# Attention products stored as high and low parts, the output projection's first units begun at step 9 of the last pair of heads, and an entrance's sum of squares kept in PSUM

## The chip, the core and the metric

One core of a Trainium2 chip. A core has a matrix engine (TensorE, PE in the profile; its weight loads are shown as PEld), three engines for elementwise work (VectorE or DVE, ScalarE or ACT, GpSimd or POOL), a queue engine (SyncE or SP), and 16 DMA engines that move data between HBM and the on-chip memories: SBUF, which holds operands, and PSUM, into which TensorE accumulates. Each engine runs its own instructions in one fixed order, and semaphores tie the engines together. The metric is the device time of one execution in microseconds (us); lower is better.

## What is computed

A decoder trunk of two layers over 1040 tokens (16 learned meta tokens and 1024 of the input) of width 1024, in float32. Layer 0 is a state-space mixer and a gated feed-forward network with a short causal convolution (conv FFN); then keys and values are projected once; layer 1 is stick-breaking attention over 16 heads and another conv FFN. The part of the reference around the change:

```
def _rmsnorm(x, g):
    x32 = x.astype(jnp.float32)
    y = x32 * lax.rsqrt(jnp.mean(x32 * x32, axis=-1, keepdims=True) + NORM_EPS)
    return (y * g.astype(jnp.float32)).astype(x.dtype)
...
        logits = jnp.einsum('bthd,bshd->bhts', q[:, t0:t1], k[:, :t1]).astype(jnp.float32) * scale
...
        log_keep = jnp.where(visible, jax.nn.log_sigmoid(-logits), 0.0)
        later = lax.cumsum(log_keep, axis=3, reverse=True) - log_keep
        log_w = jnp.where(visible, jax.nn.log_sigmoid(logits) + later, -jnp.inf)
        w = jnp.exp(log_w).astype(v.dtype)
        outs.append(jnp.einsum('bhts,bshd->bthd', w, v[:, :t1]))
...
            o = _stick_breaking_attention(q, k_shared, v_shared).reshape(b, L, SB_WIDTH)
            h = h + o @ sb_w_o[j]
        h = h + _conv_ffn(_rmsnorm(h, ffn_norm[layer]), ffn_w_up[layer], ffn_conv_w[layer],
                          ffn_conv_b[layer], ffn_w_down[layer])
```

## The kernel before

**Products in two parts.** Each float32 operand x of the large products is kept as a high part (x rounded, type F32R) and a low part (x minus the high part), and each product is three matmuls: high by high, low by high, high by low (lines 209, 210 and 211; their names, such as `acc<-o,wh`, tell what is multiplied). ScalarE makes the high part by a copy, VectorE or GpSimd the low part by a subtraction (line 102 is GpSimd's helper, which cuts a tile into pieces of 256 columns).

**Attention** runs over 8 pairs of heads; a pair has 18 steps, one for each block row i of 116 tokens and each column tile jj of 348 up to the diagonal. In a step `weigh` makes on TensorE the logits lg (line 1651), on ScalarE two sigmoids of them, kp and bt (lines 1652 and 1653), on GpSimd the masks of a diagonal block (1657), on VectorE a running product over kp (the scan, 1662) and bt times it (1663). The logits of all steps go to the same PSUM tile, so the next lg waits until ScalarE's bt has read it. Two steps later (LAG) `turn` transposes bt on TensorE (wT, 1685) and ScalarE copies it out (wt, 1691). When the block rows of a visit are through (a pair has four visits: (0, 1, 2), (3, 4, 5), (6, 7), (8,)), `values` multiplies them by v into PSUM (po, 1708), ScalarE copies po to the SBUF tile o (1710), and at three of the four visits stores o to DRAM (`o_d`, 1712) by a DMA that is issued on ScalarE's own queue. Between these, each step holds part of the next pair's projections of q, k and v (pj), whose weight parts come from ScalarE (wh, 1552) and VectorE (wl, 1553), and whose results VectorE reads (k, 1575; klo, 1587; qs, 1603; v, 1618).

**The last pair** has no next pair to project for. From its step 9 on (`BEHIND`) each step takes one piece of the generator `o_blocks`, which begins the output projection with the pairs that are done (the first four): it fetches o's rows from DRAM (`fetch_o`, line 1796, on SyncE's queue), splits them in two parts (`split_o`: ScalarE 1802, VectorE 1803), splits w_o's tiles (`parts`: ScalarE 1820, GpSimd 102), fetches rows of the residual stream h, and in `unit(f, j)` multiplies 128 output features f by token block j (12 matmuls) and adds the sum to h (VectorE, 538). The first unit stands in step 12. After the last pair the remaining units run, and `o_proj` fetches and splits the other four pairs' o for the entrance.

**An entrance** (`enter_ffn`) ends a projection and starts the FFN: for each of two token tiles it adds the last products to h, squares each of the 8 feature tiles on ScalarE (sq, 1061) and sums the squares, so that one matmul with a matrix of ones (ms) gives each token's sum. `square_row` adds them on VectorE (1063), m tiles to a sum: all in one for the first tile, none for the second. There is one entrance in each layer; the sums stand at 780 us and at 2111 us.

Of the kernel before, what the change touches and what calls it, by code (L numbers as in the profile page):

```python
# [8 lines left out]
F32 = mybir.dt.float32  # L9
F32R = mybir.dt.float32r  # L10
AF = mybir.ActivationFunctionType
ALU = mybir.AluOpType

P = 128
D = 1024
KD = D // P
META = 16
SEQ = 1024
L = META + SEQ
# [3 lines left out]
TT = [(0, 348), (348, 348), (696, 344)]  # L23
TW = 352
QW = 1056
# [35 lines left out]
PAIRS = 8  # L61
# [1 line left out]
NPOOL = 3  # L63
DT0 = 0
LAG = 2
BEHIND = 9
VISITS = (0, 1, 2), (3, 4, 5), (6, 7), (8,)

NW = 8
# [36 lines left out]
class Trunk:  # L106
# [950 lines left out]

    def square_row(self, ms, h, f, s0, n, m):

        q = self.tmp("sq")[:, :n]  # L1060
        self.nc.scalar.activation(q, h[f][:, HB + s0 : HB + s0 + n], AF.Square)
        if f % m:
            self.nc.vector.tensor_tensor(self.squares, self.squares, q, op=ALU.add)
        elif m > 1:
            self.squares = q
        if m == 1:
            self.last_ms = self.nc.tensor.matmul(ms[:, :n], self.ones, q, start=f == 0, stop=f == KD - 1, skip_group_check=True)
# [625 lines left out]
    def values(self, p, visit, wt, v, o, od):  # L1693


        nc = self.nc
        first, last = visit[0], visit[-1]
        j, c0 = first // 3, first % 3 * CB
        end = CH[last][0] + CH[last][1]
        n = end - CH[first][0]  # L1700
        each = wt[0][0].shape[1]
        po = self.ex("po")
        order = [*range(first, last + 1), *range(first - 1, -1, -1)]
        for x, c in enumerate(order):
            t0 = max(c - first, 0) * CB
            q, r = divmod(c, each)
            for a in range(2):
                nc.tensor.matmul(po[64 * a : 64 * a + 64, t0:n], v[: CH[c][1], c, 64 * a : 64 * a + 64], wt[a][q][: CH[c][1], r, t0:n],  # L1708
                                 start=x == 0, stop=x == last, skip_group_check=True)
        nc.scalar.activation(o[:, c0 : c0 + n], po[:, :n], AF.Copy)  # L1710
        if last % 3 == 2:
            nc.scalar.dma_start(od[p, :, TT[j][0] : end], o[:, : TT[j][1]])

    def attention(self, u, pool, hd):


        od = self.dp.tile([PAIRS, P, L], F32, tag="o_d", name="o_d")
        steps = [(i, jj) for i in range(9) for jj in range(i // 3, -1, -1)]

        halves = {(own, n0 + h): (kind, j, h) for own, n0, kind, j in (  # L1720
# [8 lines left out]
        def flush(n):  # L1729
            while ready:  # L1730
                p, visit = ready.pop()
                if visit[0] % 3 == 0:
                    os[p] = self.tmp("o")
                self.values(p, visit, wts.pop((p, visit)), pairs[p].v, os[p], od)
            if len(turns) > n:
                p, i, jj, bt = turns.pop(0)
                visit = next(v for v in VISITS if i in v)
                if (p, visit) not in wts:
                    wts[p, visit] = self.weight_tiles(visit)
                self.turn(i, jj, bt, wts[p, visit], visit[0])  # L1740
                if jj == 0 and i == visit[-1]:
                    ready.append((p, visit))
# [46 lines left out]
    def fetch_o(self, od, p, x):  # L1789


        g = FFN[1]
        s0, m = g.part(x)
        t = self.Q("o", F32R)
        hi, lo = t[:, :m], t[:, QW // 2 : QW // 2 + m]
        self.nc.sync.dma_start(lo.bitcast(F32), od[p, :, g.at + s0 : g.at + s0 + m])
        return hi, lo

    def split_o(self, hl):

        hi, lo = hl
        self.nc.scalar.activation(hi, lo.bitcast(F32), AF.Copy)
        self.nc.vector.tensor_tensor(lo, lo.bitcast(F32), hi.bitcast(F32), op=ALU.subtract)

    def o_blocks(self, hd, od):


        nc, a, g = self.nc, self.a, FFN[1]
        at, n, K = g.at - g.lead, g.n + g.lead, PAIRS // 2
        self.ho = h = [None] * KD  # L1810
        ws, rows = {}, [None, None]

        def fetch_w(f):
            ws[f] = self.wp.tile([P, 1024], F32, tag="w32", name=self.nm("w32"))
            nc.sync.dma_start(ws[f][:, : K * P], a["w_o_f"][f][:, : K * P])

        def parts(f):
            w32 = ws[f][:, : K * P]
            wh, wl = (self.wp.tile([P, 1024], F32R, tag=t, name=self.nm(t))[:, : K * P] for t in ("wh", "wl"))
            nc.scalar.activation(wh, w32, AF.Copy)  # L1820
            pieces(nc.gpsimd, wl, w32, wh.bitcast(F32), ALU.subtract)
            ws[f] = wh, wl

        def fetch_h(f):
            h[f] = self.Q("h")
            nc.sync.dma_start(h[f][:, :n], hd[f][:, at:])

        def unit(f, j):
            w = ws[f]
            self.accumulate(h, f, *g.span(j), lambda i, f: tuple(x[:, i * P : i * P + P] for x in w), rows[j // 2], HB, self.mm, g.part(j // 2)[0])  # L1830

        rows[0] = [self.fetch_o(od, p, 0) for p in range(K)]
        fetch_w(0)
        fetch_w(1)
        yield
        for hl in rows[0][:2]:
            self.split_o(hl)
        yield
        for hl in rows[0][2:]:
            self.split_o(hl)  # L1840
        parts(0)
        yield
        rows[1] = [self.fetch_o(od, p, 1) for p in range(K)]
        fetch_h(0)
        fetch_h(1)
        unit(0, 0)
        yield
        parts(1)
        unit(0, 1)
        yield  # L1850
        for hl in rows[1][:2]:
            self.split_o(hl)
        unit(1, 0)
        yield
        for hl in rows[1][2:]:
            self.split_o(hl)
        unit(1, 1)
        fetch_w(2)
        fetch_h(2)
        yield  # L1860
        order = [(0, 2), (0, 3), (1, 2), (1, 3)] + [(f, j) for f in range(2, KD) for j in range(4)]
        for x, (f, j) in enumerate(order):
            if x % 4 == 2 and x // 4 + 2 < KD:
                parts(x // 4 + 2)
                if x // 4 + 3 < KD:
                    fetch_w(x // 4 + 3)
                    fetch_h(x // 4 + 3)
            unit(f, j)
            yield

    def o_proj(self, od, blocks, pool):


        a = self.a
        first = PAIRS // 2
        for _ in blocks:
            pass

        def part(p, x):
            hl = self.fetch_o(od, p, x)  # L1880
            self.split_o(hl)
            return hl

        ops = [part(p, 0) for p in range(first, PAIRS)]
        ws = [self.load_wd(a["w_o"][first + i], i < 2) for i in range(4)]
        second = [part(p, 1) for p in range(first, PAIRS)]
        return self.enter_ffn(1, self.ho, [(ws, lambda: ops), (ws, lambda: second)], pool)


# [173 lines left out]
```

## Time and profile before

| what | value |
|---|---|
| three executions | 2862.64, 2856.94 and 2861.96 us; median 2861.96 us |
| profiled execution | 2864.79 us, of which the span of its instructions is 2862.9 us |
| mean granted TensorE clock | 0.996 of full speed |
| instructions | 56393 |
| ScalarE's stores of o (line 1712) | 24, 0.33 us of issue each, from 1563.9 to 2078.2 us |
| fetches of o (line 1796) | 16, of some 257 KB each, from 2014.3 to 2086.3 us |
| splits of o: ScalarE (1802), VectorE (1803) | 16 and 16, 0.63 and 0.69 us each (medians) |
| sums of squares (line 1063) | 14, of 0.43 us (median), the longest 8.88 us |

A row of the timeline reads: start in us, duration in us, engine, line, operation, what is written <- what is read, shape, how many in a row; in brackets the idle time of the engine just before it, and what it waited for. A "q" behind an engine's name is its sequencer, which issues DMAs. A row of windows gives, for a stretch of time, its length and the busy us (and instructions) of PE, PEld, DVE, ACT and POOL, the granted clock of TensorE, the busy share of the DMA engines and GB/s. A row of one line's instructions gives least/median/greatest duration in ns. A row of waits gives who waits, for whom, us in total, times, and the longest.

### The profile page before, as it was taken

Reading aid. Unit: us, or ns where it says so; the run is one execution under the profiler, and the core shown is the slowest. Engines: PE = TensorE matmul, PEld = TensorE weight load, DVE = VectorE, ACT = ScalarE, POOL = GpSimd, SP = SyncE. Lnnn points to the kernel's source line nnn. Section 1 sums busy time; section 2 is a strip of 40 time slices with the busy share of each in tenths; the row PEclk is TensorE's granted clock in tenths of the full one; section 3 lists DMA queues with packets and bytes.
Section 4 is the critical chain, followed back from the end, with each engine's and each line's share of the span. In section 5 each row is a group of like instructions: output and inputs, shape, how many; then the busy total and the mean of one; then the engine's idle time right before and its main releaser. Section 6 shows DMA issues by size and latency. Waiting matters only on the chain.

```text
span 2862.9 us, 56393 instructions
## 1 busy us (share of the span) xinstructions
PE 2813.9 (98%) x21251; PEld 2695.1 (94%) x21251; DVE 2073.6 (72%) x3920; ACT 1589.3 (56%) x3093; POOL 1577.6 (55%) x2144
## 2 busy tenths in 40 slices
PE   8999999999999999999999999999899999999998
PEld 7989999999999999999999999999799999999888
DVE  5676666668597666677886888878669776766776
ACT  5555454543265656555335777777636555555433
POOL 2366455643529888868853111122254888885881
PEclk9999999999999999999999999999999999999999
DMA  4343334333413222245132222221432222225331
GB/s 119 88 112 103 107 86 134 108 132 101 126 59 97 81 79 79 80 156 174 43 128 77 66 69 62 63 59 47 136 107 76 80 80 78 81 82 184 111 104 67
DMA packets 136237, 273.32 MB, mean 95 GB/s; under 512 B 15924, under 2 KB 68285, under 8 KB 135965
## 3 DMA queue, kind: packets, MB, share of 16 engines
q1 hardware_dynamic: 130340, 258.55, 28.9%
q0 software_dynamic: 2048, 6.49, 0.6%
q10 hardware_dynamic: 3576, 4.67, 0.5%
q8 instruction: 168, 2.75, 0.4%
q14 instruction: 105, 0.85, 0.1%
HBM read 203.58 MB, written 51.16 MB: 89 GB/s over the span
## 4 chain that ended last, share of the span: by engine, by line
PE 89%; DVE 5%; ACT 2%; issue 2%; POOL 1%; DMA 0%; DVEq 0%; SPq 0%; ACTq 0%; POOLq 0%
PE p L211 10%; PE p L209 10%; PE p L210 10%; PE acc L209 8%; PE acc L211 8%; PE acc L210 8%; PE pj L209 8%; PE pj L210 7%; PE pj L211 7%; PE po L1708 2%; PE lg L1651 2%; PE wT L1685 2%; PE y L810 1%; PE S L799 1%; PE y L812 1%
## 5 line engine op out<-in xcount | busy, mean ns | idle before, releaser
L102 POOL TENSOR_TENSOR wl<-w,wh 128x256 fp32r<-128x256 f32 x760 | 678.9, 923 | 359.8 <-ACT wh L196 216.8
L209 PE MATMUL pj<-uh,wh 128*128 128x348 f32 (+2 forms) x1536 | 500.7, 327 | 2.1 <-DVE xbc L339 1.4
L210 PE MATMUL pj<-ul,wh 128*128 128x348 f32 (+2 forms) x1536 | 494.8, 322 | 0.8 <-DVE ul L320 0.8
L211 PE MATMUL pj<-uh,wl 128*128 128x348 f32 (+2 forms) x1536 | 492.1, 320 | 0.0
L209 PE MATMUL p<-bh,fh 128*128 128x262 f32 (+1 forms) x1408 | 400.8, 285 | 3.9 <-DVE p L1235 3.7
L211 PE MATMUL p<-bh,fl 128*128 128x262 f32 (+1 forms) x1408 | 400.8, 285 | 2.0 <-POOL fl L102 2.0
L210 PE MATMUL p<-bl,fh 128*128 128x262 f32 (+1 forms) x1408 | 397.5, 283 | 0.0
L102 POOL TENSOR_TENSOR fl<-x,fh 128x256 fp32r<-128x256 f32 x352 | 263.9, 782 | 190.3 <-ACT fh L1172 140.0
L210 PE MATMUL p<-bl,wh 128*128 128x262 f32 (+1 forms) x1040 | 295.5, 284 | 0.7 <-DVE bl L1096 0.7
L209 PE MATMUL p<-bh,wh 128*128 128x262 f32 (+1 forms) x1040 | 295.2, 284 | 0.8 <-ACT ft L1232 0.8
L211 PE MATMUL p<-bh,wl 128*128 128x262 f32 (+1 forms) x1040 | 294.3, 283 | 0.0
L209 PEld LDWEIGHTS pj<-uh,wh 128*128 128x128 f32 x1536 | 288.7, 188 | 4.5 <-ACT xbc L336 1.7
L210 PEld LDWEIGHTS pj<-ul,wh 128*128 128x128 f32 x1536 | 289.3, 188 | 2.4 <-DVE ul L320 1.4
L339 DVE SCALAR_TENSOR_TENSOR c<-p,params,c 128x260 f32<-128x260 f32 (+1 forms) x528 | 248.2, 479 | 57.5 <-ACT c L336 50.9
L211 PEld LDWEIGHTS pj<-uh,wl 128*128 128x128 f32 x1536 | 288.7, 188 | 0.1
L209 PEld LDWEIGHTS p<-bh,fh 128*128 128x128 f32 x1408 | 267.8, 190 | 4.8 <-DVE p L1235 4.1
L211 PEld LDWEIGHTS p<-bh,fl 128*128 128x128 f32 x1408 | 265.9, 189 | 2.9 <-POOL fl L102 2.7
L210 PEld LDWEIGHTS p<-bl,fh 128*128 128x128 f32 x1408 | 267.4, 190 | 0.1
L1232 ACT ACTIVATE ft<-p 128x262 f32<-128x262 f32 (+1 forms) x352 | 133.2, 382 | 178.9 <-DVE p L1235 110.9
L210 PE MATMUL acc<-gl,wh 128*128 128x260 f32 (+1 forms) x672 | 214.1, 320 | 0.0
L211 PE MATMUL acc<-gh,wl 128*128 128x260 f32 (+1 forms) x672 | 213.4, 320 | 0.0
L209 PE MATMUL acc<-gh,wh 128*128 128x260 f32 (+1 forms) x672 | 210.7, 320 | 0.1
(337 smaller groups left out, 7712.8 us busy)
## 6 DMA issues: line engine op xcount, KB each, us to landing
w<-in_w_up SPq DMA_DIRECT2D x88, 512.0 KB
w<-in_w_down SPq DMA_DIRECT2D x44, 512.0 KB
w<-in_w_in SPq DMA_DIRECT2D x40, 512.0 KB
E<-ea_d SPq DMA_DIRECT2D x32, 464.0 KB
D<-acs_d SPq DMA_DIRECT2D x32, 420.5 KB
g<-c SPq DMA_DIRECT2D x88, 130.0 KB
g<-c SPq DMA_DIRECT2D x88, 128.0 KB
b<-g SPq DMA_DIRECT2D x16, 520.0 KB
```

The lines of the kernel that those rows point to most:

```text
L102: done.append(eng.tensor_tensor(out[:, c], x[:, c], y[:, c], op=op))
L209: self.behind(mm(out, wh, uh, start=first, stop=False, skip_group_check=joins), tie, "behind the sums of squares")
L210: mm(out, wh, ul, start=False, stop=False, skip_group_check=joins)
L211: self.last_mm = mm(out, wl, uh, start=False, stop=last, skip_group_check=joins)
L339: ins = nc.vector.scalar_tensor_tensor(out, ps[:, o + i : o + i + n], wcol(i), out, op0=ALU.mult, op1=ALU.add)
L799: nc.tensor.matmul(ps, bk[:n], xde[:n].rearrange("p h d -> p (h d)"), start=True, stop=True)
L810: nc.tensor.matmul(y, xdt[:n, i, :], dk[:, i, :], start=True, stop=c == 0)
L812: nc.tensor.matmul(y, state[:, i, :], ce[:, i, :], start=False, stop=True)
L1232: nc.scalar.activation(s[:, :N], ps[:, :N], AF.Copy)
L1651: nc.tensor.matmul(ps[:nt, a, :m], part[:, c0 : c0 + nt], ks[a][:, s0 : s0 + m], start=x == 0, stop=x == 1)
L1685: nc.tensor.transpose(pt[:ns, x * CB : x * CB + nt], bt[:nt, a, x * CB : x * CB + ns], self.ident[:nt, :nt])
L1708: nc.tensor.matmul(po[64 * a : 64 * a + 64, t0:n], v[: CH[c][1], c, 64 * a : 64 * a + 64], wt[a][q][: CH[c][1], r, t0:n], start=x == 0, st ...
```

## The change

Three things. **First**, `values` makes two tiles of po, hi (ScalarE's copy, rounded) and lo (a new subtraction on VectorE, po - hi), and stores both, hi and then lo, on ScalarE's queue: 48 stores in place of 24, with `o_d` twice as large. `fetch_o` fetches both parts (32 fetches in place of 16), and `split_o` is gone (16 instructions on ScalarE and 16 on VectorE; 32 come on VectorE). **Second**, `BEHIND` is 5, and the pieces of `o_blocks` are dealt out anew: step 5 fetches the first rows of o and two tiles of w_o, steps 6 and 7 split these, step 8 fetches rows of h, and the first unit stands in step 9, so that nine units stand in the last pair in place of six. **Third**, in `square_row` the first square of a tile that is summed goes to a PSUM tile, where the sum stays; the last addition writes to SBUF, from which the matmul with ones takes it.

```
--- before.py
+++ after.py
@@ -63,7 +63,7 @@
 NPOOL = 3
 DT0 = 0
 LAG = 2
-BEHIND = 9
+BEHIND = 5
 VISITS = (0, 1, 2), (3, 4, 5), (6, 7), (8,)
 
 NW = 8
@@ -1057,11 +1057,13 @@
 
     def square_row(self, ms, h, f, s0, n, m):
 
-        q = self.tmp("sq")[:, :n]
+        q = self.sm("sq")[:, :n] if m > 1 and f == 0 else self.tmp("sq")[:, :n]
         self.nc.scalar.activation(q, h[f][:, HB + s0 : HB + s0 + n], AF.Square)
-        if f % m:
-            self.nc.vector.tensor_tensor(self.squares, self.squares, q, op=ALU.add)
-        elif m > 1:
+        if m > 1:
+            if f:
+                out = q if f == m - 1 else self.squares
+                self.nc.vector.tensor_tensor(out, self.squares, q, op=ALU.add)
+                q = out
             self.squares = q
         if m == 1:
             self.last_ms = self.nc.tensor.matmul(ms[:, :n], self.ones, q, start=f == 0, stop=f == KD - 1, skip_group_check=True)
@@ -1707,14 +1709,17 @@
             for a in range(2):
                 nc.tensor.matmul(po[64 * a : 64 * a + 64, t0:n], v[: CH[c][1], c, 64 * a : 64 * a + 64], wt[a][q][: CH[c][1], r, t0:n],
                                  start=x == 0, stop=x == last, skip_group_check=True)
-        nc.scalar.activation(o[:, c0 : c0 + n], po[:, :n], AF.Copy)
+        hi, lo = (x[:, c0 : c0 + n] for x in o)
+        nc.scalar.activation(hi.bitcast(F32R), po[:, :n], AF.Copy)
+        nc.vector.tensor_tensor(lo.bitcast(F32R), po[:, :n], hi, op=ALU.subtract)
         if last % 3 == 2:
-            nc.scalar.dma_start(od[p, :, TT[j][0] : end], o[:, : TT[j][1]])
+            for x, t in enumerate(o):
+                nc.scalar.dma_start(od[p, x, :, TT[j][0] : end], t[:, : TT[j][1]])
 
     def attention(self, u, pool, hd):
 
 
-        od = self.dp.tile([PAIRS, P, L], F32, tag="o_d", name="o_d")
+        od = self.dp.tile([PAIRS, 2, P, L], F32, tag="o_d", name="o_d")
         steps = [(i, jj) for i in range(9) for jj in range(i // 3, -1, -1)]
 
         halves = {(own, n0 + h): (kind, j, h) for own, n0, kind, j in (
@@ -1730,7 +1735,7 @@
             while ready:
                 p, visit = ready.pop()
                 if visit[0] % 3 == 0:
-                    os[p] = self.tmp("o")
+                    os[p] = [self.tmp("o") for _ in range(2)]
                 self.values(p, visit, wts.pop((p, visit)), pairs[p].v, os[p], od)
             if len(turns) > n:
                 p, i, jj, bt = turns.pop(0)
@@ -1792,15 +1797,10 @@
         g = FFN[1]
         s0, m = g.part(x)
         t = self.Q("o", F32R)
-        hi, lo = t[:, :m], t[:, QW // 2 : QW // 2 + m]
-        self.nc.sync.dma_start(lo.bitcast(F32), od[p, :, g.at + s0 : g.at + s0 + m])
-        return hi, lo
-
-    def split_o(self, hl):
-
-        hi, lo = hl
-        self.nc.scalar.activation(hi, lo.bitcast(F32), AF.Copy)
-        self.nc.vector.tensor_tensor(lo, lo.bitcast(F32), hi.bitcast(F32), op=ALU.subtract)
+        hl = t[:, :m], t[:, QW // 2 : QW // 2 + m]
+        for y, q in enumerate(hl):
+            self.nc.sync.dma_start(q.bitcast(F32), od[p, y, :, g.at + s0 : g.at + s0 + m])
+        return hl
 
     def o_blocks(self, hd, od):
 
@@ -1833,38 +1833,34 @@
         fetch_w(0)
         fetch_w(1)
         yield
-        for hl in rows[0][:2]:
-            self.split_o(hl)
-        yield
-        for hl in rows[0][2:]:
-            self.split_o(hl)
         parts(0)
         yield
-        rows[1] = [self.fetch_o(od, p, 1) for p in range(K)]
+        parts(1)
+        fetch_w(2)
+        yield
         fetch_h(0)
         fetch_h(1)
+        yield
+        rows[1] = [self.fetch_o(od, p, 1) for p in range(K)]
+        fetch_h(2)
         unit(0, 0)
         yield
-        parts(1)
         unit(0, 1)
         yield
-        for hl in rows[1][:2]:
-            self.split_o(hl)
         unit(1, 0)
         yield
-        for hl in rows[1][2:]:
-            self.split_o(hl)
         unit(1, 1)
-        fetch_w(2)
-        fetch_h(2)
+        parts(2)
+        fetch_w(3)
+        fetch_h(3)
         yield
         order = [(0, 2), (0, 3), (1, 2), (1, 3)] + [(f, j) for f in range(2, KD) for j in range(4)]
         for x, (f, j) in enumerate(order):
-            if x % 4 == 2 and x // 4 + 2 < KD:
-                parts(x // 4 + 2)
-                if x // 4 + 3 < KD:
-                    fetch_w(x // 4 + 3)
-                    fetch_h(x // 4 + 3)
+            if x % 4 == 2 and x // 4 + 3 < KD:
+                parts(x // 4 + 3)
+                if x // 4 + 4 < KD:
+                    fetch_w(x // 4 + 4)
+                    fetch_h(x // 4 + 4)
             unit(f, j)
             yield
 
@@ -1876,14 +1872,9 @@
         for _ in blocks:
             pass
 
-        def part(p, x):
-            hl = self.fetch_o(od, p, x)
-            self.split_o(hl)
-            return hl
-
-        ops = [part(p, 0) for p in range(first, PAIRS)]
+        ops = [self.fetch_o(od, p, 0) for p in range(first, PAIRS)]
         ws = [self.load_wd(a["w_o"][first + i], i < 2) for i in range(4)]
-        second = [part(p, 1) for p in range(first, PAIRS)]
+        second = [self.fetch_o(od, p, 1) for p in range(first, PAIRS)]
         return self.enter_ffn(1, self.ho, [(ws, lambda: ops), (ws, lambda: second)], pool)
 
 
```

Where rows move, as the compiled programs' order has them (line, operation, what is written <- what is read, size; x4 means four in a row; the numbers behind names are those of buffers). On ScalarE, in the third pair of heads at visit (0, 1, 2), before:

```order
L1653 ACTIVATE bt_20496<-lg_20498,rt_18459 116x2x348
L1586 ACTIVATE k_19558<-k_20473 128x344
L1552 ACTIVATE wh_20475<-w_2655_20434,params 128x128 x4
L1710 ACTIVATE o_20535<-po_20536 128x348
L1712 DMA o_d<-o_20535 128x348
L1691 ACTIVATE wt_20546<-wT_20549 116x116
L1691 ACTIVATE wt_20548<-wT_20552 116x116
L1652 ACTIVATE kp_20555<-lg_20558,rt_18460 116x2x348
L1653 ACTIVATE bt_20556<-lg_20558,rt_18459 116x2x348
```

and now:

```order
L1655 ACTIVATE bt_20516<-lg_20518,rt_18459 116x2x348
L1588 ACTIVATE k_19568<-k_20493 128x344
L1554 ACTIVATE wh_20495<-w_2661_20454,params 128x128 x4
L1713 ACTIVATE o_20555<-po_20557 128x348
L1717 DMA o_d<-o_20555 128x348
L1717 DMA o_d<-o_20556 128x348
L1693 ACTIVATE wt_20569<-wT_20572 116x116
L1693 ACTIVATE wt_20571<-wT_20575 116x116
L1654 ACTIVATE kp_20578<-lg_20581,rt_18460 116x2x348
L1655 ACTIVATE bt_20579<-lg_20581,rt_18459 116x2x348
```

A second store, of the tile lo (o_20556), stands between the first store and the copies wt; it waits for the instruction that writes lo. That one stands on VectorE; at the same place of the program VectorE had

```order
L1663 TENSOR_TENSOR bt_20496<-bt_20496,kp_20495 116x2x348
L1587 TENSOR_TENSOR klo_20521<-k_20473,k_19558 128x344
L1553 SCALAR_TENSOR_TENSOR wl_20476<-w_2655_20434,params,wh_20475 128x128 x4
L1662 SCALAR_TENSOR_TENSOR kp_20555<-kp_20555,one 116x349 x2
L1663 TENSOR_TENSOR bt_20556<-bt_20556,kp_20555 116x2x348
```

and has now, with visit (3, 4, 5) of the same pair behind the line of dots:

```order
L1665 TENSOR_TENSOR bt_20516<-bt_20516,kp_20515 116x2x348
L1589 TENSOR_TENSOR klo_20541<-k_20493,k_19568 128x344
L1555 SCALAR_TENSOR_TENSOR wl_20496<-w_2661_20454,params,wh_20495 128x128 x4
L1714 TENSOR_TENSOR o_20556<-po_20557,o_20555 128x348
L1664 SCALAR_TENSOR_TENSOR kp_20578<-kp_20578,one 116x349 x2
...
L1605 TENSOR_TENSOR qs_20848<-pj_20736,qs_20848 64x348
L1605 TENSOR_TENSOR qs_20850<-pj_20736,qs_20850 64x348
L1714 TENSOR_TENSOR o_20857<-po_20858,o_20856 128x348
L1664 SCALAR_TENSOR_TENSOR kp_20885<-kp_20885,kp_20818,one 116x349 x2
L1665 TENSOR_TENSOR bt_20886<-bt_20886,kp_20885 116x2x348
```

The subtraction lo (line 1714) stands behind what the step has given VectorE already: the four wl products at the first visit, the two qs subtractions at the second. The third place is VectorE in the last pair, around the first units' sums (line 538); before:

```order
L1803 TENSOR_TENSOR o_24968<-o_24968 128x514
L1803 TENSOR_TENSOR o_24970<-o_24970 128x514
L1662 SCALAR_TENSOR_TENSOR kp_25023<-kp_25023,kp_24990,one 116x349 x2
L1663 TENSOR_TENSOR bt_25024<-bt_25024,kp_25023 116x2x348
L1803 TENSOR_TENSOR o_24972<-o_24972 128x514
L1803 TENSOR_TENSOR o_24974<-o_24974 128x514
L1662 SCALAR_TENSOR_TENSOR kp_25063<-kp_25063,one 116x233 x2
L1663 TENSOR_TENSOR bt_25064<-bt_25064,kp_25063 116x2x232
L538 TENSOR_TENSOR h_25088<-h_25088,acc_25092 128x258
```

and now:

```order
L1664 SCALAR_TENSOR_TENSOR kp_25045<-kp_25045,one 116x117 x2
L1665 TENSOR_TENSOR bt_25046<-bt_25046,kp_25045 116x2x116
L1620 TENSOR_TENSOR v_24248<-pv_25062,rt_18458 116x384
L538 TENSOR_TENSOR h_25033<-h_25033,acc_25087 128x258
L1664 SCALAR_TENSOR_TENSOR kp_25111<-kp_25111,kp_25045,one 116x349 x2
L1665 TENSOR_TENSOR bt_25112<-bt_25112,kp_25111 116x2x348
L538 TENSOR_TENSOR h_25033<-h_25033,acc_25130 128x256
```

The splits (line 1803) are gone from between the scans, and the first sum of a unit stands three steps earlier.

## The prediction

> **What bounds the kernel now.** I read the page's busy shares, then its chain of waits, then windows of the stages that the change touches, then single rows of the timeline there (rows between those shown are left out).
>
> ```profile
> PE 2813.9 (98%) x21251; PEld 2695.1 (94%) x21251; DVE 2073.6 (72%) x3920; ACT 1589.3 (56%) x3093; POOL 1577.6 (55%) x2144
> ...
> PE 89%; DVE 5%; ACT 2%; issue 2%; POOL 1%; DMA 0%; DVEq 0%; SPq 0%; ACTq 0%; POOLq 0%
> ...
> 1900.00:2000.00 100.00, 99.12 (x749) 91.19 (x748) 83.78 (x143) 74.97 (x179) 18.95 (x53) 1.00 0.22 58
> 2030.00:2040.00 10.00, 8.69 (x40) 4.94 (x40) 5.38 (x7) 1.77 (x5) 3.42 (x6) 0.66 0.39 131
> 2050.00:2060.00 10.00, 6.94 (x53) 6.29 (x52) 9.63 (x14) 5.97 (x14) 1.28 (x5) 1.00 0.01 2
> 2120.00:2130.00 10.00, 7.72 (x38) 7.37 (x39) 5.84 (x16) 4.96 (x11) 2.50 (x5) 0.66 0.41 132
> ```
>
> TensorE is the bound: 98% busy, 89% of the chain. So an edit is worth what it adds to or takes from TensorE's idle time and granted clock. In the middle pairs of heads (1900 to 2000) there is next to nothing to take: TensorE is busy for 99.12 of 100 us, VectorE for 84, ScalarE for 75. The holes are in the last pair (2030 to 2060) and in the second entrance (2120 to 2130), and two of these three 10-us windows also ran at a granted clock of 0.66. The change works at these two thin places, and puts its new work into the full one.
>
> **The stores: what the middle pairs pay.** Each visit gets one VectorE subtraction (lo = po - hi) and, at three of a pair's four visits, a second store on ScalarE's queue, behind the first and ahead of the next weight copies. It reads lo, so it waits for VectorE. Visit (0, 1, 2) of the third pair, as it runs now:
>
> ```profile
> 1692.82 0.41 PE L1685 MATMUL wT<-ident,bt 116*116 116x116 f32 x2
> 1692.94 0.46 ACT L1710 ACTIVATE o<-po 128x348 f32<-128x348 f32 x1
> 1693.43 0.33 ACTq L1712 DMA_DIRECT2D o_d<-o  x1
> 1693.81 0.43 ACT L1691 ACTIVATE wt<-wT 116x116 f32<-116x116 f32 x2 [0.40 <-ACT o L1710]
> 1694.84 0.86 ACT L1653 ACTIVATE bt<-lg,rt 116x696 f32<-116x696 f32 x1
> 1695.27 1.39 DVE L1553 SCALAR_TENSOR_TENSOR wl<-w,params,wh 128x128 fp32r<-128x128 f32 x4
> 1695.60 0.76 PE L1685 MATMUL wT<-ident,bt 116*116 116x116 f32 x6
> 1696.13 0.87 PE L1651 MATMUL lg<-k,qs 128*116 128x348 f32 x4
> ```
> ```profile
> L1575 DVE TENSOR_TENSOR k<-pj,r x24: 505/517/522, 1524.8 to 1999.6; 128x348 f32<-128x348 f32 x16, 128x344 f32<-128x344 f32 x8
> ```
>
> First, a store on ScalarE's queue holds ScalarE: wT was ready at 1692.82 + 0.41 = 1693.23, yet its copy wt began only at 1693.81, behind the store, with ScalarE idle for 0.40. Second, VectorE is behind: in the changed order lo stands behind the four wl products, and these end at 1695.27 + 1.39 = 1696.66, 3.26 us after ScalarE's copy of po (1693.40). The trace has no such subtraction; its price I take from the nearest row, L1575, a TENSOR_TENSOR of 348 columns with one operand in PSUM: 0.51 (this row's least and most are 0.505 and 0.522, so its bounds change nothing). So lo ends at 1697.17; with the spacings of the rows (0.03 to the store, 0.33 its issue, 0.05 to wt) wt begins at 1697.58, **3.77 us late**. The copies kp and bt follow wt, and TensorE's next lg overwrites what bt reads: bt ended at 1695.70, lg began at 1696.13, so 0.43 is slack, and **3.34 us of TensorE are lost**. TensorE has nothing to fill them with: its order is fixed, and the next rows in it, wT and lg, are those that wait.
>
> Visit (3, 4, 5) of the same pair:
>
> ```profile
> 1715.30 0.33 ACTq L1712 DMA_DIRECT2D o_d<-o  x1
> 1715.73 0.42 ACT L1691 ACTIVATE wt<-wT 116x116 f32<-116x116 f32 x2 [0.46 <-PE lg L1651]
> 1716.04 1.06 DVE L1603 TENSOR_TENSOR qs<-pj,qs 64x348 fp32r<-64x348 f32 x2
> 1716.76 0.85 ACT L1653 ACTIVATE bt<-lg,rt 116x696 f32<-116x696 f32 x1
> 1717.99 0.88 PE L1651 MATMUL lg<-k,qs 128*116 128x348 f32 x4
> ```
>
> There lo stands behind qs, which ends at 1717.10. So lo ends at 1717.61, wt begins at 1718.02 instead of 1715.73, 2.29 late; bt's end moves from 1717.61 to 1719.90, and lg, which began at 1717.99, loses **1.91 us**. Visit (6, 7) stores nothing, and visit (8) finds VectorE free:
>
> ```profile
> 1749.50 1.78 DVE L1662 TENSOR_TENSOR_SCAN kp<-kp,kp,one 116x349 f32<-116x349 f32 x2 [2.65 <-ACT kp L1652]
> ...
> 1952.15 0.33 ACTq L1712 DMA_DIRECT2D o_d<-o  x1
> 1953.99 1.39 DVE L1553 SCALAR_TENSOR_TENSOR wl<-w,params,wh 128x128 fp32r<-128x128 f32 x4
> 1974.01 0.33 ACTq L1712 DMA_DIRECT2D o_d<-o  x1
> 1974.75 1.06 DVE L1603 TENSOR_TENSOR qs<-pj,qs 64x348 fp32r<-64x348 f32 x2
> ```
>
> VectorE was idle for 2.65 there, so lo waits for nobody, and the second store shifts ScalarE by its issue alone, 0.33, less than the 0.43 of slack above; I cost it at nothing (at most 7 x 0.33 = 2.3). The other rows are the seventh pair's: from the store's begin to the end of wl 3.23 us, as in the third pair (1696.66 - 1693.43), and to the end of qs 1.80, as there. So seven pairs pay alike: 7 x (3.34 + 1.91) = **+36.8 us**. From below: TensorE's first stall gives VectorE time to catch up, so the second may vanish, 7 x 3.34 = 23.4; and nothing if the store does not hold ScalarE. From above, the clock: both are rivals below.
>
> **The last pair.** Its visit (0, 1, 2) pays too:
>
> ```profile
> 2015.20 0.42 ACT L1691 ACTIVATE wt<-wT 116x116 f32<-116x116 f32 x2 [0.40 <-ACT o L1710]
> 2015.45 0.88 DVE L1663 TENSOR_TENSOR bt<-bt,kp 116x696 f32<-116x696 f32 x1
> 2017.14 0.89 PE L1651 MATMUL lg<-k,qs 128*116 128x348 f32 x4 [0.35 <-ACT bt L1653]
> 2029.71 0.39 PE L209 MATMUL acc<-o,wh 128*128 128x258 f32 x1 [1.22 <-ACT wh L1820]
> 2032.40 0.58 PE L210 MATMUL acc<-o,wh 128*128 128x258 f32 x1 [1.01 <-DVE o L1803]
> 2053.32 0.39 PE L210 MATMUL acc<-o,wh 128*128 128x256 f32 x1 [2.04 <-DVE o L1803]
> 2060.68 0.39 PE L209 MATMUL acc<-o,wh 128*128 128x256 f32 x1 [1.58 <-DVE h L538]
> ```
>
> lo follows VectorE's bt (2016.33) and ends at 2016.84, wt begins at 2017.25 instead of 2015.20, and lg already waits, so all **+2.0 us** show. Against it stand gains. The splits of o (L1803) are gone, and w_o's first parts are made three steps ahead of the first unit, so 1.22 + 1.01 + 2.04 go; the 1.58 for a sum h, which VectorE reaches late behind splits and bt products, goes with them. The window 2030 to 2040 loses 10 x (1 - 0.66) = 3.4 us by its clock, right behind the first two waits; without them it keeps its clock. Sum 9.25; the earlier units meet VectorE in three more steps, for which I take back 0.25: **-9.0 us**. The bounds are -12 (the three further units also fill small waits for bt like the 0.35) and -4 (only the splits' own waits and half of the rest go).
>
> What the steps issue besides:
>
> ```profile
> 2000.00:2100.00 100.00, 90.73 (x724) 81.33 (x723) 62.48 (x98) 54.43 (x113) 32.44 (x57) 0.97 0.43 139
> ```
> ```profile
> L1796 SPq DMA_DIRECT2D o<-o_d x16: 320/382/991, 2014.3 to 2086.3; - x16
> ```
>
> SyncE issues 16 more fetches, 16 x 0.38 = 6.1 us of its queue, where no arithmetic stands; the first rows are asked for four steps before the first unit, as the later rows are before theirs, and the DMA engines are busy to 0.43 in this window, so twice o's bytes find room. GpSimd, 32 of 100 us busy, makes wl earlier, between two steps' masks. Both at nothing; if the first rows came late, the first unit would wait as it does now (1.22 and 1.01 above), which is within the bound of -4.
>
> **The entrance's squares.**
>
> ```profile
> 2111.41 10.47 DVE L1063 TENSOR_TENSOR sq<-sq,sq 128x258 f32<-128x258 f32 x4
> 2114.42 5.59 POOL L102 TENSOR_TENSOR fl<-x,fh 128x256 fp32r<-128x256 f32 x8
> 2122.28 0.58 PE L209 MATMUL acc<-o,w 128*128 128x256 f32 x1 [3.98 <-DVE h L538]
> ```
> ```profile
> L538 DVE TENSOR_TENSOR h<-h,acc x192: 404/420/519, 681.4 to 2854.0; 128x256 f32<-128x256 f32 x72, 128x260 f32<-128x260 f32 x56, 128x348 f32<-128x348 f32 x32, 128x344 f32<-128x344 f32 x16
> ```
>
> Four sums of squares take 10.47 us while GpSimd runs without a gap, and TensorE waits 3.98 us for the sum h behind them. L538, with one operand in PSUM, never took over 0.52 in 192 times, whatever GpSimd did. With its sum in PSUM, L1063 has the same mixture, so I take L538's 0.42 for each, and the stall goes. The clock of 0.66 that follows costs up to 3.4 in its window, 2120 to 2130; but TensorE stands there until 2122.28, and at half speed 2.28 / 2 = 1.1 of the loss falls into idle time: 3.98 + 2.3 = **-6.3 us** (from -3, if half stays, to -7.4, if all 3.4 counts). The first entrance's sums lie under a busy TensorE: nothing.
>
> **The sum.** The profiled execution took 2864.79 us (span 2862.9), 2.83 above the median of the runs. 2864.79 + 36.8 + 2.0 - 9.0 - 6.3 = 2888.3; on the scale of the median 2885.5, so **2885 us**, about 0.8% slower.
>
> **The rule on the clock.** After waits of 1.22 and 1.01 within 4 us the clock fell to 0.66 (window 2030 to 2040); after one of 2.04 it did not (2050 to 2060: 1.00). A stall of 3.34, cut by one wT, is nearer to the first. The Trainium skill, "TensorE: Matmul & The Clock Gate", Part 1, says that the array's clock halves after at least one whole idle window of about 3.4 us; by that rule a stall with a wT in its middle would keep the clock, and the sum would stay 2885. The rows above disagree: less idle time was enough.
>
> **Rivals.**
> - **The clock falls at each first stall.** Price as in 2030 to 2040, 3.4 each, while VectorE catches up in that time, so that the second stall goes: 7 x (3.34 + 3.4) = 47.2 in place of 36.8, **2896**. For it: what follows the row 2032.40; against it: 2053.32. 0.20.
> - **The second stall vanishes**, because TensorE's first loss lets VectorE's queue run empty before visit (3, 4, 5): 23.4 in place of 36.8, **2872**. Against it: VectorE's scan behind lo needs kp, which is late by as much. 0.14.
> - **The gains don't come**: the units in the last pair wait for doubled fetches, or the PSUM sums are held up as the others were: 6.3 to 9 less, **2893**. For it: transfers take 0.43 of the queues here; against it: the rows of L538. 0.12.
> - **Faster than before: the store does not hold ScalarE**, because a wait on its queue lets later copies pass. Then each pair pays lo's 0.51 on VectorE alone, 3.6 in all, and 2864.8 + 3.6 - 9.0 - 6.3 - 2.8 gives **2850**. Against it: the idle 0.40 of 1693.81 with wT done. It decides where the hold costs TensorE less than (9.0 + 6.3 - 2.0) / 7 = 1.9 us a pair. The Trainium skill, "Perfetto Trace Analysis", DMA Instruction — HWDGE, puts a store's semaphore wait into the issuing engine's sequencer, ahead of its next instruction, and so against this rival; the 0.40 agrees. 0.10.
>
> **How the numbers follow.** The forecast itself has 0.44. The range, 2867 to 2904, takes in its bounds, the clock's case and the lost gains, and the second stall's vanishing; it leaves out the fast rival and clock losses on top of both stalls (2909). A measurement of this kernel can tell some 0.2%, 5.7 us, from no change. Nearly all of the fast rival gives faster, 0.09; its rest and the weak end of the vanishing stall lie between 2856 and 2868, 0.05; slower has 0.86.
>
> **What would show it.** In the changed profile: ScalarE's wt behind a visit's second store idle for over 3 us, waiting for VectorE's lo; TensorE's waits for bt, now these in 1540 to 2000,
>
> ```profile
> PE lg L1651 <- ACT bt L1653: 2.6, 7, 0.7
> ```
>
> become fourteen of some 3 and 2 us; a 100-us window of the middle pairs falls from 99 to about 92 busy; granted clock of 0.66 in windows there would be the clock's rival. The four sums at 0.42, and no 3.98 and no 2.04, show the gains. If ScalarE runs wt right behind the first store, the forecast is wrong by all of 36.8.

## The result, and the profile after

| | before | changed |
|---|---|---|
| executions, median (least to greatest) | 2862.30 us (2856.94 to 2862.75), 4 | 2896.14 us (2894.27 to 2897.65), 4 |
| ratio, 95% interval | | 1.0122 (1.0105 to 1.0140) |
| profiled execution, its span | 2864.79 us, 2862.9 us | 2897.65 us, 2895.7 us |
| mean granted clock | 0.996 | 0.990 |

The change costs 1.2%, 33.8 us by the medians. The forecast was 2885 us, in a range of 2867 to 2904. The page's first lines of the changed kernel, its busy shares and its chain:

```profile
PE 2829.9 (98%) x21251; PEld 2709.3 (94%) x21251; DVE 2070.0 (71%) x3936; ACT 1581.6 (55%) x3077; POOL 1564.5 (54%) x2144
...
PE 84%; DVE 8%; issue 3%; ACT 2%; POOL 1%; DMA 0%; ACTq 0%; DVEq 0%; POOLq 0%
```

TensorE has the same instructions; its share of the chain fell from 89 to 84%, and VectorE's rose from 5 to 8. Windows of the changed kernel (columns as explained above), first the middle pairs, then the last pair's first visit, then the entrance:

```profile
1900.00:2000.00 100.00, 92.52 (x676) 85.31 (x675) 76.68 (x134) 67.37 (x161) 15.36 (x51) 0.94 0.23 62
...
2060.00:2070.00 10.00, 7.28 (x36) 6.58 (x35) 7.01 (x8) 6.07 (x13) 5.45 (x9) 0.70 0.37 102
...
2150.00:2160.00 10.00, 10.00 (x85) 10.00 (x84) 6.19 (x16) 5.86 (x13) 10.00 (x16) 1.00 0.64 195
```

Where 99.12 of 100 us were busy, 92.52 are, and the clock there fell from 1.00 to 0.94. The entrance, a hole before, is full. What TensorE waits for between 1540 and 2010 us of the changed kernel, and who waits for the new subtraction (its line's own view):

```profile
PE wT L1687 <- ACT wt L1693: 13.4, 7, 2.2
PE lg L1653 <- ACT bt L1655: 12.8, 16, 1.1
```
```profile
  ACT wt L1693: 40.9, 14
```

Before, the waits for bt were 2.6 us in all, and wT never waited for wt. In the whole execution ScalarE's copies wt now wait 40.9 us in 14 places for the subtraction o (line 1714): at the first visit of all eight pairs (3.2 to 4.2 us each) and at the second visit of six (1.5 to 1.6). The third pair's first visit, from the timeline of the changed kernel:

```profile
1705.33 0.44 ACT L1713 ACTIVATE o<-po 128x348 fp32r<-128x348 f32 x1
1705.80 3.95 ACTq L1717 DMA_DIRECT2D o_d<-o  x2
...
1707.83 1.13 DVE L1555 SCALAR_TENSOR_TENSOR wl<-w,params,wh 128x128 fp32r<-128x128 f32 x4
1708.88 0.51 DVE L1714 TENSOR_TENSOR o<-po,o 128x348 fp32r<-128x348 f32 x1
1709.79 0.43 ACT L1693 ACTIVATE wt<-wT 116x116 f32<-116x116 f32 x2 [4.03 <-DVE o L1714]
1710.12 0.51 PE L1687 MATMUL wT<-ident,bt 116*116 116x116 f32 x3 [2.16 <-ACT wt L1693]
...
1711.44 1.80 DVE L1664 TENSOR_TENSOR_SCAN kp<-kp,one 116x349 f32<-116x349 f32 x2 [2.05 <-POOL kp L1659]
1711.73 1.03 PE L1653 MATMUL lg<-k,qs 128*116 128x348 f32 x4 [1.11 <-ACT bt L1655]
```

The two stores together occupy 3.95 us of ScalarE's queue: the first is issued at once, the second when VectorE, behind its four wl products, has written lo at 1709.39. ScalarE stands for 4.03 us, TensorE first for wt (2.16) and then for bt (1.11): 3.27 us. Over the seven pairs the first of these two waits is 1.79 to 2.17 us, the second 1.11 each time. And VectorE itself waits 2.05 us behind lo, since its next scan needs the kp that ScalarE was kept from. The same pair's second visit:

```profile
1731.98 1.40 ACTq L1717 DMA_DIRECT2D o_d<-o  x2
1732.49 0.52 DVE L1714 TENSOR_TENSOR o<-po,o 128x348 fp32r<-128x348 f32 x1
1733.48 0.43 ACT L1693 ACTIVATE wt<-wT 116x116 f32<-116x116 f32 x2 [1.53 <-DVE o L1714]
...
1735.42 0.89 PE L1653 MATMUL lg<-k,qs 128*116 128x348 f32 x4 [0.52 <-ACT bt L1655]
```

Here only 0.52 us is left of the loss: lo ends at 1733.01, 1.03 us after the stores begin, where the prediction had 2.31 (1717.61 - 1715.30). Where the rest went stands in the clock between the two visits:

```profile
1710.00:1720.00 10.00, 8.78 (x51) 8.50 (x52) 8.22 (x16) 8.62 (x23) 2.19 (x8) 0.83 0.26 75
1720.00:1730.00 10.00, 10.00 (x75) 9.11 (x75) 9.73 (x21) 9.22 (x22) 1.15 (x5) 1.00 0.28 81
```

TensorE loses 10 x (1 - 0.83) = 1.7 us behind the first stall. VectorE, 9.73 of the next 10 us busy, has caught up by the second visit. Over the seven pairs the two rows of waits rise from 2.6 to 26.2 us, 23.6 more, and the granted clock between 1563 and 2060 us is 0.96, another 20 us: together they are nearly all that the pairs lose. The entrance's sums and the last pair, as they now run:

```profile
2060.23 3.15 ACTq L1717 DMA_DIRECT2D o_d<-o  x2
...
2063.74 0.72 PE L1687 MATMUL wT<-ident,bt 116*116 116x116 f32 x3 [1.82 <-ACT wt L1693]
...
2065.36 1.51 PE L1653 MATMUL lg<-k,qs 128*116 128x348 f32 x4 [0.90 <-ACT bt L1655]
...
2152.64 1.98 DVE L1065 TENSOR_TENSOR sq<-sq,sq 128x258 f32<-128x258 f32 x4
```

Four sums in 1.98 us where 10.47 stood, while GpSimd is busy all the time (window 2150 to 2160 above), and no wait of 3.98 behind them.

To put the stages side by side, the traces of all kernels are cut at four instructions: ScalarE's copy of po at the first visit of the first and of the eighth pair, the end of the last po, and the end of the last matmul with o. In us, worked out from the timelines' starts:

| kernel | seven pairs | last pair | last po to last o | rest behind |
|---|---|---|---|---|
| before | 450.97 | 63.55 | 85.87 | 699.14 |
| changed | 496.35 | 63.56 | 74.84 | 697.54 |
| stores_only | 497.12 | 58.71 | 85.26 | 698.08 |
| sq_only | 451.20 | 63.28 | 79.20 | 699.19 |
| sp_store | 454.44 | 60.74 | 74.84 | 697.84 |
| late_store | 455.01 | 60.83 | 74.84 | 697.53 |
| sp_store_b9 | 454.48 | 55.83 | 79.10 | 698.06 |
| one_store | 451.85 | 61.21 | 76.53 | 697.63 |
| fill | 491.11 | 63.85 | 74.84 | 697.70 |

So in the traces the change costs 45.4 us in the seven pairs and gains 11.0 behind the last one (and 1.6 later). Each row is one execution. Three more of the kernel before (below) show how far a column moves by itself: the first from 450.97 to 451.08, the second from 62.04 to 63.55, the last from 698.02 to 699.18, so that most of the 1.6 may be no gain of the change. In the trace a unit moved into the last pair moves 1.44 us (12 matmuls of 0.12) from the third column to the second.

### The profile page after: what moved, and what is told of

It is laid out like the page before. It is cut to its first block, busy times and chain, and to the rows that moved or that the text cites. A ratio compares the mean times of both kernels' runs of the same rounds, so it can differ in the third digit from the quotient of the medians.

```text
span 2895.7 us, 56474 instructions
## 1 busy us (share of the span) xinstructions
PE 2829.9 (98%) x21251; PEld 2709.3 (94%) x21251; DVE 2070.0 (71%) x3936; ACT 1581.6 (55%) x3077; POOL 1564.5 (54%) x2144
## 4 chain that ended last, share of the span: by engine, by line
PE 84%; DVE 8%; issue 3%; ACT 2%; POOL 1%; DMA 0%; ACTq 0%; DVEq 0%; POOLq 0%
PE p L209 10%; PE p L211 10%; PE p L210 10%; PE acc L209 8%; PE acc L211 8%; PE acc L210 8%; PE pj L209 7%; PE pj L210 7%; PE pj L211 7%; DVE kp L1664 2%; PE lg L1653 2%; PE po L1710 1%; PE wT L1687 1%; PE y L810 1%; DVE wl L1555 1%
```

## The experiments

The theory: the second store's wait for lo, on ScalarE's queue, holds ScalarE and through it TensorE. The rivals: that the subtractions and the doubled bytes themselves cost the time; and, on the size, that the clock's fall is a cost of its own.

**The third part alone (sq_only).** The kernel before with

```
-        q = self.tmp("sq")[:, :n]
+        q = self.sm("sq")[:, :n] if m > 1 and f == 0 else self.tmp("sq")[:, :n]
...
+                out = q if f == m - 1 else self.squares
```

> The kernel before with the third part alone: the sum of an entrance's first tile stays in PSUM. If sums with an operand in PSUM aren't held up by GpSimd's burst, the four sums at 2111 us take 0.42 us each in place of 10.47 in all, TensorE's wait of 3.98 us and the low clock behind it go, and the time is 6 to 7 us below before, near 2856. If they are held up all the same, the time stays at 2862 and the 10.47 stands in the trace.

Measured: 2857.17 us against 2858.73 of before on the same chip, ratio 0.9992 (0.9982 to 1.0003). The trace does what was expected (the third column falls by 6.7), and the sums are never held up again; the view of their line:

```profile
L1065 DVE TENSOR_TENSOR sq<-sq,sq x14: 426/435/438, 780.1 to 2116.2; 128x260 f32<-128x260 f32 x7, 128x258 f32<-128x258 f32 x7
```

But the medians differ by 1.6 us only, and the interval takes in no change at all: a miss by 4 to 5 us. The reason is in the kernel before: its 29 executions lie between 2855.32 and 2868.28, 15 of them at 2858.73 or less, 14 at 2861.08 or more, while 11 of sq_only's 12 lie between 2855.81 and 2858.06. To see what parts them, the kernel before was profiled three times more.

> The kernel before, once more, for its trace: its executions on this chip lie in two groups, 2855 to 2859 and 2861 to 2868. If the sum of squares that took 8.88 us in its first trace takes that long in some executions only, a profiled execution of the lower group has no 10.47 us row at the second entrance and no wait of 3.98, and one of the upper group has both.

> The kernel before for another trace. The one profiled last took 2861.65 us, of the upper group, with the wait of 3.9 us at the second entrance. If the stall of the sum of squares is what parts the groups, an execution of 2855 to 2859 us shows no such wait, and the sums near 0.43 to 0.9 us each.

> As the run before it: the stall with a time of 2861 us and more, none with a time below 2859. A lower time with the stall in the trace, or a higher one without it, would speak against the sum as what parts the groups.

before_look1 took 2861.65 us, before_look2 2862.96, before_look3 2862.08. The first two have the wait behind the sums (3.9 and 4.1 us). The sums' line in the first and in the third:

```profile
L1063 DVE TENSOR_TENSOR sq<-sq,sq x14: 422/432/8793, 780.4 to 2122.8; 128x260 f32<-128x260 f32 x7, 128x258 f32<-128x258 f32 x7
```
```profile
L1063 DVE TENSOR_TENSOR sq<-sq,sq x14: 429/770/939, 780.2 to 2122.4; 128x260 f32<-128x260 f32 x7, 128x258 f32<-128x258 f32 x7
```

The same program, the same burst of GpSimd: one execution has a sum of 8.79 us, the other none over 0.94, and TensorE never waits there (third column 79.18 instead of 84.96). So the stall that the prediction priced is not in every execution. It is not the only thing that varies, either: before_look3 without the stall took as long as the others, because its attention began 5 us later (its first copy of po at 1568.64, of the others at 1563.4 to 1563.6). Its trace has the reason in layer 0's FFN, in another addition of VectorE whose operands all lie in SBUF:

```profile
875.69 5.57 DVE L1235 TENSOR_TENSOR ft<-ft,ft 128x262 f32<-128x262 f32 x1
```

The median of these additions is 0.79 us. GpSimd is busy beside it until 880.98, nearly to its end, and TensorE waits 3.9 us for what ScalarE makes behind it. So a hold-up of the same kind stands at another place: late_store has it there too (5.56 us, its attention begins at 1568.46), and before, before_look2 and sq_only have one of 5.2 us in layer 1's FFN; the table's last column is 1.1 us longer in these three than in before_look1 and before_look3. No execution of the lower group was profiled, so that these hold-ups part the groups is not shown.

**The first part alone (stores_only).** The changed kernel with `BEHIND = 9`, the steps of before (without splits), and the sums in SBUF.

> The first part alone: two stores and two fetches, no splits, but the units from step 12 and the sums in SBUF as before. By the theory that the second store holds ScalarE, with the low clock behind each first stall, the middle pairs take 6.5 us more each (45 us over seven), the last pair's first visit another 5, less some 3 for the splits' waits: near 2909. By the rival that the moved units or the PSUM sums also cost something, it is faster than the changed kernel's 2896.

Measured: 2902.04 us (2898.46 to 2907.21), ratio 1.0153 (1.0135 to 1.0171). The seven pairs cost what they cost in the changed kernel (497.12 and 496.35). The total is 7 us under what was expected, in the traces all of it in the last pair: 58.71, when 63.55 less 3 for the splits, and 5 more for the hold, had been assumed. It is not faster than the changed kernel, as it would be if the other two parts had cost something.

**The second store elsewhere (sp_store).**

```
-                nc.scalar.dma_start(od[p, x, :, TT[j][0] : end], t[:, : TT[j][1]])
+                (nc.scalar, nc.sync)[x].dma_start(od[p, x, :, TT[j][0] : end], t[:, : TT[j][1]])
```

> The changed kernel with the second store (of lo) on SyncE's queue; the subtraction, the bytes, the moved units and the PSUM sums are as in the changed kernel. If the wait of that store on ScalarE's queue is the cause, the seven first-visit stalls and the low clock behind them go, and the time is 2848 to 2854. If VectorE's 32 subtractions or the doubled bytes are the cause, it stays near 2896. If SyncE, held in its place, brings the copies of q and k late, it lies between, with TensorE waiting for a DMA.

Measured: 2854.92 us (2851.86 to 2860.49), ratio 0.9986 (0.9977 to 0.9996), 0.9 above what was expected; the changed kernel's loss is gone with one word. TensorE's window and its waits between 1540 and 2010 in sp_store:

```profile
1900.00:2000.00 100.00, 98.77 (x746) 90.63 (x745) 85.80 (x153) 74.76 (x178) 18.05 (x50) 1.00 0.24 65
```
```profile
PE lg L1653 <- ACT bt L1655: 4.4, 7, 0.7
PE wT L1687 <- DVE v L1620: 1.7, 4, 1.0
```

No wait for wt, no DMA among the waits, full clock. All subtractions and all bytes are still there, and cost 454.44 - 450.97 = 3.5 us in seven pairs, 0.5 a pair: what is left of the rival.

**The second store later (late_store).** The store of lo stays on ScalarE's queue, but is issued at the next step's `flush`:

```
+            self.pending = lambda: nc.scalar.dma_start(od[p, 1, :, TT[j][0] : end], lo)
...
         def flush(n):
+            if self.pending:
+                self.pending()
+                self.pending = None
```

> The changed kernel with the second store left on ScalarE's queue, but issued one step later, behind that step's kp and bt. By the theory its wait shrinks: at the first visit from 3.4 us to some 1 us, at the second to nothing, so TensorE loses about 1 us a pair, too little for the clock to fall: 2855 to 2860. If it is the store's issue as such (0.33 us) or the bytes that cost, it stays near 2896.

Measured: 2854.07 us (2851.52 to 2858.82), ratio 0.9982 (0.9971 to 0.9992), 0.9 under what was expected. The wait of wt for lo did not vanish, but shrank: between 1540 and 2010 us it is 36.0 us in 12 places in the changed kernel, and in late_store (the second row is TensorE's wait):

```profile
ACT wt L1693 <- DVE o L1714: 9.5, 7, 1.7
```
```profile
PE lg L1653 <- ACT bt L1655: 4.5, 7, 0.9
```

A hold of some 1.4 us instead of 4.0 leaves TensorE one wait of at most 0.9 a pair, and its clock stays. So it is neither the queue nor the issue, but how long the store that stands there waits.

**The stall without the low clock (fill).** In `half`, for the projection that runs just ahead of each first-visit stall, with a tile of zeros:

```
+                    if (kind, j, h, parts, k) == ("v", 2, 1, 2, KD - 1):
+                        for _ in range(12):
+                            nc.tensor.matmul(ps[:, :n], self.nil, u[k][0][:, o:e], start=False, stop=False)
```

> The changed kernel with 12 matmuls by zeros added to the projection that TensorE runs just ahead of each first-visit stall in the first seven pairs (1.9 us a pair; they add zeros and change no value). The stall as such stays, since it is ScalarE that is late; the matmuls only fill its first part. If the low clock behind the stalls costs what its stretches say (20 us of full speed over seven pairs), the clock stays at 1.00 there, the second stalls come back by some 1.4 us each, and the time falls from 2896 to some 2884 to 2888. If the clock's fall costs nothing of its own, the added matmuls gain nothing: 2896 or more.

Measured: 2895.64 us (2892.88 to 2897.91), ratio 1.0124 (1.0109 to 1.0138): by the times no gain, a miss. The trace says why. Windows and waits between 1540 and 2010 of fill:

```profile
1700.00:1800.00 100.00, 96.08 (x708) 87.40 (x708) 82.54 (x154) 72.53 (x178) 17.13 (x53) 1.00 0.25 69
1900.00:2000.00 100.00, 96.14 (x730) 89.02 (x729) 79.69 (x145) 70.54 (x172) 17.48 (x54) 1.00 0.22 62
```
```profile
PE lg L1656 <- ACT bt L1658: 14.8, 14, 1.3
PE wT L1690 <- ACT wt L1696: 3.4, 8, 0.5
```

The clock is full in these windows (in two others, 1660 to 1670 and 2010 to 2020, it is 0.83, behind second visits), and the second stalls are back, fourteen waits for bt instead of one large and one small a pair. At the third pair's second visit lo now ends at 1732.75, 2.12 us after the stores begin (1.03 in the changed kernel):

```profile
1730.63 2.49 ACTq L1720 DMA_DIRECT2D o_d<-o  x2
```

The seven pairs take 491.11 us, 5.2 less than in the changed kernel. The medians don't bear this out, they are 0.5 us apart: the profiled execution of fill is the shortest of its four, that of the changed kernel the longest. But the trace of stores_only shows the same inside one execution. Two of its pairs have equal first stalls (1.8 and 1.1 us); their windows, the second pair's and the fourth's:

```profile
1636.00:1646.00 10.00, 7.08 (x50) 6.58 (x49) 7.71 (x14) 7.08 (x19) 1.73 (x5) 1.00 0.31 100
1779.00:1789.00 10.00, 7.10 (x32) 6.58 (x29) 7.65 (x16) 6.35 (x15) 1.22 (x4) 0.66 0.33 90
```

Where the clock stayed up, the second visit's waits are 0.5 and 1.3 us and the pair takes 70.31 us; where it fell, which costs 3.4 us there, one wait of 0.6 is left and the pair takes 72.24. So the low clock behind a stall is in part a swap: of the 3.4 us that TensorE loses by it, 1.9 are left in the pair's time, since VectorE has caught up before the next visit.

**Are the moved units worth anything?** sp_store_b9 is sp_store with `BEHIND = 9` and the steps of before without splits; one_store is sq_only with the units from step 9, one store, and the splits in steps 6, 7, 10 and 11.

> The kernel with the second store on SyncE's queue, but the units from step 12 as before. By the trace of the PSUM sums alone, moving the units is worth some 7 us, 2.7 in the last pair and 4.3 behind it, so this one is near 2860. If it was the splits' going that helped, and the earlier start adds nothing, it stays at 2854 to 2855.

> The second and third parts without the first: units from step 9 and PSUM sums, but one store of o and the splits (in steps 6, 7, 10 and 11). If moving the units is what gains in and behind the last pair, and the two-part store is not needed for it, 2850 to 2851, as the subtractions' 0.5 us a pair is saved too. If the splits stand in the units' way wherever they are, TensorE waits for them again (3 us and the low clock behind): 2855 to 2857, as with the PSUM sums alone.

Measured: sp_store_b9 2853.44 us (2852.74 to 2855.21), ratio 0.9975 (0.9966 to 0.9984); one_store 2854.41 us (2853.16 to 2855.63), ratio 0.9981 (0.9971 to 0.9990), which lies between its two expectations. For sp_store_b9 the first one, 2860, was wrong: without the moved units sp_store loses nothing. Its last pair is 4.9 us shorter and the stage behind it 4.3 longer, which is the three units' 4.3 changing places. What sq_only's last pair waits for and these two don't, between 2010 and 2110 us of sq_only, of sp_store_b9 and of one_store:

```profile
PE acc L210 <- DVE o L1805: 3.1, 2, 2.0
...
PE acc L209 <- ACT wh L1822: 1.2, 1, 1.2
```
```profile
PE acc L209 <- DVE h L538: 1.9, 2, 1.6
PE lg L1653 <- ACT bt L1655: 1.7, 6, 0.4
```
```profile
PE acc L209 <- DVE h L538: 5.9, 5, 2.0
PE lg L1653 <- ACT bt L1655: 3.2, 4, 1.4
```

The splits just ahead of their units are what cost time in the last pair. In it and the stage behind it, against sq_only's 142.48 us, their going gains 7.5 (sp_store_b9: 134.93), and making them three steps earlier 4.7 (one_store: 137.74), since there TensorE meets sums h on VectorE instead (5.9). Over the whole kernel the two come to nearly the same, because one_store has no subtractions to pay in the seven pairs. sp_store_b9, one_store and late_store all beat the kernel before by about 0.2%, and can't be told apart.

## Why the prediction was right, point by point

The direction and the range held. The forecast itself, 2885, is 11 us short: of the two mechanisms that the text put side by side, the rival's took place.

- **TensorE as the bound, and the full place as the one that pays**: right. Its wait and clock in the middle pairs decide the time.
- **The store that holds ScalarE at the first visit**: right in place and size. 3.34 us of TensorE were forecast, 2.16 + 1.11 = 3.27 measured in the third pair, and 2.9 to 3.3 in all seven; the four wl products stand ahead of lo as read from the order. sp_store shows it: the same work without that wait on ScalarE's queue takes 454 us in place of 496.
- **The second visit, 1.91**: 0.52 measured in the third pair, since the clock fell behind the first stall. With the clock kept (fill) it comes back, at 1.4 to 1.8. 36.8 us for both over seven pairs were forecast; the seven pairs cost 45.4. This is the term that was mis-sized, and the traces divide it: (491.11 - 454.44) / 7 = 5.24 a pair for the stalls at nearly full clock (fill against sp_store, where fill's added matmuls count as stall, since they fill it; 5.25 was forecast), 3.5 us for the subtractions and the doubled bytes, which the sum had left at nothing and only the fast rival had priced (3.6), and 5.2 for the clock, of one trace each.
- **The rival of the clock**: it is what happened. It gave 47.2 for the seven pairs, by trading the second stall for a low clock, and 2896; measured are 45.4 and 2896.14. That the sums agree to a fraction of a us is luck, as several terms are off by 1 to 2 us and cancel. It had a chance of 0.20 and should have had more than that: a stall of 3.3 us was nearer to the row after which the clock fell than to the row after which it didn't, as the text itself said. And the row against it was that of one execution: behind the same wait of 2.04 us the clock did fall in before_look1 and before_look2 (0.83 from 2050 to 2060), and again not in before_look3. The Trainium skill's rule, "TensorE: Matmul & The Clock Gate", Part 1, of a whole idle window, would have kept the clock; here 1.79 to 2.17 us of idle, wT, and 1.11 more were enough in all seven pairs of the changed kernel.
- **The rival that the second stall vanishes by TensorE's first loss alone**: fell. Where the clock stayed up (fill, and stores_only's second pair) it is there, 1.4 to 1.8 us.
- **The rival that the gains don't come**: fell. Behind the seven pairs the traces gain 11.0 us, and TensorE waits for no fetch in the last pair.
- **The rival that the store holds nobody**: fell. The Trainium skill, "Perfetto Trace Analysis", DMA Instruction — HWDGE, has the wait in the issuing engine's sequencer, and the trace agrees: 4.03 us of ScalarE behind it.
- **The last pair, +2.0 and -9.0**: the hold costs 63.56 - 60.74 = 2.8 there (changed kernel against sp_store). The gain, from sq_only to sp_store over the last pair and the stage behind it, is 142.48 - 135.58 = 6.9, so the 9.0 was 2.1 too large. It comes from the splits' going; that units stand there earlier gives nothing on top of that (sp_store_b9).
- **The entrance, -6.3**: 6.7 in the traces. But the stall is not in each execution of the kernel before, so the median gains less (sq_only: 1.6). A forecast on the scale of the medians should not have taken it whole. On the scale of the traces the forecast was 2888.3 and 2897.65 was measured, 9.4 more. Of this 8.6 lie in the seven pairs; the errors behind them (hold, gain and entrance) and the 1.6 that nobody forecast leave 0.8.

## What to carry to other kernels

Here a store that was issued from ScalarE's queue held ScalarE for as long as the store's operand was late, 4.03 us, though the operand's producer takes 0.51; so look up what stands ahead of the producer on its own engine, not how long the producer takes. On a queue that nobody computes on, or a step later, the same work cost 3.5 to 4.0 us over seven pairs in place of 45.4. A stall that is followed by a low clock need not be dearer by all that the clock loses, when another engine is behind and uses the time. And a row of one execution, of a wait or of the clock, may not be there in the next.

## What was not expected of the hardware

One and the same program, with the same neighbours in time, had a VectorE addition of two SBUF operands take 8.79 to 9.02 us beside GpSimd's burst in three profiled executions, and 0.94 at the most in a fourth, which had one of 5.57 us elsewhere; stores_only, with its sums in SBUF too, had 9.05. With one operand in PSUM, none of these sums took over 0.44 in any run.

The clock fell to half speed behind all seven first stalls of the changed kernel, idle times of 1.79 to 2.17 and 1.11 us with 0.51 us of work between them. Idle time of this size doesn't settle it: behind 1.81 and 1.11 it stayed up once in stores_only, and in fill it stayed up behind 0.26 and 1.11 but fell behind 0.53 and 1.31 and behind 0.50 and 1.11. What else decides is open.
